# Output products of the dilated heads: one goes from the third latent pair to the last, and the last pair's three are tied to places in TensorE's order

## The chip, the cores and the metric

One core of a Trainium2 chip runs the kernel. The metric is device time in microseconds (us) of one execution. Engines are named as the profile names them: PE is TensorE (PEld its weight loads), DVE is VectorE, ACT is ScalarE, POOL is GpSimd, SP is SyncE.

## What is computed

A trunk of two layers over 512 tokens of width 1024. Each layer computes, in float32 (cut from the reference):

```python
h = rms_norm(x, g_norm_mix) * (1 + sc1) + sh1
q_d, k_d, v_d, cq, ckv, k_rope = split(h @ w_in)
o_dil = dilated_attention(...)      # 8 heads
o_mla = latent_attention(...)       # 8 heads
mix = concatenate([o_dil, o_mla]) @ w_out
x = x + gt1 * mix
h = rms_norm(x, g_norm_mlp) * (1 + sc2) + sh2
x = x + gt2 * (square(relu(h @ w_mlp_in)) @ w_mlp_out)
```

`x` is held transposed, as eight tiles `xT[j]` of 128 rows and 512 tokens. The product with `w_out` falls into a dilated half (the first 512 rows of `w_out`) and a latent half, and each half into eight output tiles j.

## The kernel before

**Precision.** A float32 weight tile is loaded into a `raw` buffer by SP's queue, copied by ACT to a rounded high part (`wh`), and POOL subtracts that from `raw` to give the low part `wl` (`load_split`, L229 to L238). A product of two such pairs is three matmuls: high by high, low by high, high by low (`mm3`, L240 to L245). There are 3 `raw`, 4 `wh` and 4 `wl` buffers, and 4 PSUM banks under the tag `mm`, 2 under `sc` and 2 under `tr`.

**Heads.** A layer runs its 16 heads as eight pairs, in the loop over `st` (0 to 7). Pairs 0 to 3 are dilated, pairs 4 to 7 latent; "third latent pair" is `st` 6, "last pair" `st` 7. `head` (L332 to L382) works through four query blocks: scores on TensorE, the maximum on DVE (L353), the exponential on ACT (L354), a normalising step that is on ACT (L358) for two blocks and on POOL (L362) for the other two, four transposes on TensorE (L365), and copies of the turned block by ACT (L370) and DVE (L371). After the four blocks comes the value product (L377), whose result ACT and DVE take out (L380, L381). At the end of a pair its output is split into `OT[st]` by ACT and POOL (L662, L663). While a pair runs, the queries, keys and values of the next pair are projected, normalised and transposed (`tail`, L636 to L645).

**Output products.** `out_dil(j)` (L697) is the whole dilated half of output tile j: four inner steps k of three matmuls each, 12 matmuls of 512 columns into one `mm` bank, and then a residual add of 512 columns on DVE (`add_x`, L670). It reads `OT[0]` to `OT[3]` (tiles named `ot` and `h` in the profile) and the weight tile `wo[0, j // 2]`; a weight tile serves two j. `early(j)` (L689) is the part of the latent half, on the first 256 tokens, that doesn't need the last pair: nine matmuls of 256 columns. The rest of the latent half follows when the last pair is done, then the norm, then the MLP.

**The order of the work.** The code traces the instructions in an order, and a planner then issues them: it walks a simulated time line, and on each engine takes, of the instructions that are ready, the one that was traced first. `heads` yields after each query block and after the value product, so five times for a head. `weave` (L708) fires the events of a pair between these yields: an event with position p fires at the first yield whose count i is greater than p. For `st` of 4 and more, `out_dil(2 * (st - 4))` stands at position 3.1 and `out_dil(2 * (st - 4) + 1)` at 5.1 (`OD0`, `OD1` in `TUNE`). The weight tiles of the dilated half are loaded at the end of the pairs 3 to 6 (`LO`, 7.2), those of the latent half in the last pair between 0.5 and 5 (`OL0`, `OL1`). `early(0)`, `early(1)` and `early(2)` stand at 5.5, 6.5 and 7.5 of the last pair, and `early(3)` to `early(6)` hang on hooks in its second head.

These positions give an instruction its rank, not its place. A place is fixed by `tc.keep_in_program_order(ins)`: it adds an edge from `ins` to the instruction of the same engine that was traced just before it, so that `ins` is issued behind that one. `mm3` does this for its first matmul where `pin` is true; `out_lat` and `early` pass it on for their first inner step.

In layer 0 the same stretch also carries blocks of the conditioning product (`mod_block`, L162 to L172) on DVE, or on POOL and ACT, which use `raw` buffers too.

Of the kernel before, what the change touches and what calls it, by code (L numbers as in the profile page):

```python
# [42 lines left out]
def trunk(ctx: ExitStack, tc: tile.TileContext, a):  # L43
    nc = tc.nc
    tn = lambda k: TUNE[k][min(lay[0], len(TUNE[k]) - 1)]
# [27 lines left out]
    def ps(tag, shape=(128, 512)):  # L73
        return psum.tile(list(shape), F32, tag=tag, bufs=BUFS[tag], name=nm(tag))
# [37 lines left out]
    for i in range(2):  # L112
        p = ps("sc", (128, 4, 128))
# [99 lines left out]
    def next_mod(**kw):  # L213
        if modq:
            modq.pop(0)(**kw)
# [24 lines left out]
    def mm3(out, sh, sl, mh, ml, first, last, pin=False):  # L240
        r = T.matmul(out, sh, mh, start=first, stop=False)  # L241
        if pin:
            tc.keep_in_program_order(r)
        T.matmul(out, sl, mh, start=False, stop=False)  # L244
        T.matmul(out, sh, ml, start=False, stop=last)  # L245
# [142 lines left out]
    for l in range(L):  # L388
# [6 lines left out]
        OT = []  # L395
# [259 lines left out]
        def heads(st, w):  # L655
            pr, bias = st % 4, (bias0 if l == 0 else True) if st < 4 else None
            o = s2(tag="o")
            for hd in range(2):
                hook = (lambda at: [early(j) for j in EARLY[at]]) if st == 7 and hd else (lambda at: None)
                yield from head(l, 2 * pr + hd, hd, w["score"], bias, w["vals"], o, hook)  # L660
            ot = t4("h" if st in (2, 3) else "ot", [128, 2, S])
            A.activation(ot[:, 0], o, AF.Copy)  # L662
            G.tensor_tensor(ot[:, 1], o, f(ot[:, 0]), op=OP.subtract)  # L663
            OT.append(ot)
# [4 lines left out]
        def add_x(j, hf, p, gt):  # L669
            V.scalar_tensor_tensor(xT[j][:, hf], p, gt[:, j:j + 1], xT[j][:, hf], op0=OP.mult, op1=OP.add)  # L670
# [3 lines left out]
        def out_load(half, jj):  # L674
            hi, lo = load_split(a["wout"][l, half, jj], 1024, tags=("zz", "zz") if half and jj == 3 else ("wh", "wl"))
            wo[half, jj] = (hi.rearrange("p (j k m) -> p j k m", j=2, k=4), lo.rearrange("p (j k m) -> p j k m", j=2, k=4))
# [12 lines left out]
        def early(j, pin=True):  # L689
            p = ps("mm")[:, :256]  # L690
            out_lat(j, p, HALF[0], (0, 1, 2), True, j < 4, pin)
            if j < 4:
                add_x(j, HALF[0], p, gt1)
            else:
                held[j] = p

        def out_dil(j):  # L697
            wh, wl = wo[0, j // 2]
            p = ps("mm")
            for k in range(4):  # L700
                mm3(p, wh[:, j % 2, k], wl[:, j % 2, k], OT[k][:, 0], OT[k][:, 1], k == 0, k == 3)
            add_x(j, slice(0, S), p, gt1)

        def run(events):
# [3 lines left out]
        def weave(main, events):  # L708
            ev = sorted(events, key=lambda x: x[0])
            i = 0  # L710
            for _ in main:
                i += 1
                while ev and ev[0][0] < i:
                    ev.pop(0)[1]()
            for _, fn in ev:
                fn()

        def spread(fns, p0, p1):
            return [(p0 + (p1 - p0) * i / max(1, len(fns) - 1), fn) for i, fn in enumerate(fns)]

        def flow(w, p0, p1):

            d = (p1 - p0) / 4
            ev = []
            for tb in range(4):
                b0 = p0 + d * tb
                ev += spread(w["mm"][tb], b0, b0 + 0.9 * d) + [(b0 + 0.95 * d, w["chain"][tb])]
            return ev
# [5 lines left out]
        if l == 0:  # L734
# [3 lines left out]
            p = ps("sc")  # L738
# [55 lines left out]
        else:  # L794
# [6 lines left out]
            ev = []  # L801
# [4 lines left out]
        for st in range(8):  # L806
            ev = []
            nx = PR.get(st + 1)
            if st == 0:
                if l == 0:  # L810
                    ev += spread(PR[1]["load"][2:], -2, -1)
                else:
                    ev += spread(PR[1]["load"], -2, -1)
            if st < 3:
                ev += flow(nx, tn("F0"), tn("F1")) + [(tn("T0"), nx["tail"][0]), (tn("T1"), nx["tail"][1])]
            elif nx:
                ev += flow(nx, tn("M0"), tn("M1")) + [(tn("M2"), nx["tail"][0]), (tn("M3"), nx["tail"][1])]
            if st < 2:
                ev += spread(PR[st + 2]["load"], tn("LD0"), tn("LD1"))
            elif st < 6:  # L820
                ev += [(tn("LM"), PR[st + 2]["load"][0])]
            if st >= 3 and st < 7:
                ev += [(tn("LO"), lambda jj=st - 3: out_load(0, jj))]
            if st >= 4:
                ev += [(tn("OD0"), lambda j=2 * (st - 4): out_dil(j)), (tn("OD1"), lambda j=2 * (st - 4) + 1: out_dil(j))]
            if st == 7:
                ev += spread([lambda jj=jj: out_load(1, jj) for jj in range(4)], tn("OL0"), tn("OL1"))
                ev += [(tn("OE") + j, lambda j=j: early(j)) for j in range(3)]
            if l == 0:
                on_dve = ("MV0", "MV1", "MV2", "MV3") if st < 3 else ("MV4", "MV5") if 4 <= st < 7 else ()  # L830
                on_pool = ("MP0", "MP1") if 4 <= st < 7 else ()
                ev += [(tn(x), lambda: next_mod(pin=True)) for x in on_dve]
                ev += [(tn(x), lambda: next_mod(pool_=True)) for x in on_pool]
            weave(heads(st, PR[st]), ev)
# [10 lines left out]
        for j in (4, 5, 6, 7, 0, 1, 2, 3):  # L845
            p = held[j] if j >= 4 else ps("mm")[:, :256]
# [4 lines left out]
        for j in range(8):  # L851
            p = ps("mm")[:, :256]
# [27 lines left out]
        for grp in ((0, 8), (8, 16), (16, 24), (24, 28), (28, 32)):  # L880
# [19 lines left out]
            if grp[1] - grp[0] == 8:  # L900
                for j in range(8):
                    w = tuple(t.rearrange("p (k m) -> p k m", k=8) for t in load_split(a["w2a"][l, grp[0] // 8, j], 1024))
                    p = ps("mm")
# [4 lines left out]
            else:  # L908
                gi = (grp[0] - 24) // 4
                ws = []  # L910
                for hf in ((FULL,) if gi == 0 else HALF):
                    n = hf.stop - hf.start
                    for j in range(8):
# [4 lines left out]
                        p = ps("mm")[:, :n]  # L918
# [70 lines left out]
```

## Time and profile before

| | |
|---|---|
| median of 3 runs | 1345.82 us (1344.32 to 1347.77) |
| profiled execution | 1343.71 us |
| its span, first to last instruction | 1341.6 us |
| PE, PEld busy | 1263.8 us (94%), 1108.2 us (83%) |
| DVE, ACT, POOL busy | 762.4, 679.8, 652.0 us |

The profile is one execution. Its time and its span differ by what lies around the first and the last instruction. Busy times of matmuls overlap a little, since they are pipelined: a busy PE is one that has no gap, and the distance between starts tells what one matmul takes.

### The profile page before, as it was taken

The numbers are of one execution on the slowest core, as the hardware profiler recorded it, in microseconds if no ns is written. First come the engines' busy times: TensorE is split into PE (matmuls) and PEld (weight loads), VectorE is DVE, ScalarE is ACT, GpSimd is POOL, SyncE is SP. The second block draws the span as 40 slices with busy tenths as digits, with TensorE's granted clock in tenths as the row PEclk, the third lists the DMA queues.
The fourth block names the chain that finished last, engine by engine and source line by source line (L and its number), as shares of the span: only waits on it lengthen the run. The fifth ranks groups of instructions, "written<-read, shape, count | busy, mean of one in ns | idle before, by whom it ended". The sixth has DMA issues, their size and how long they took to land.

```text
span 1341.6 us, 19641 instructions
## 1 busy us (share of the span) xinstructions
PE 1263.8 (94%) x7114; PEld 1108.2 (83%) x7114; DVE 762.4 (57%) x1644; ACT 679.8 (51%) x1421; POOL 652.0 (49%) x504
## 2 busy tenths in 40 slices
PE   4879988988999999999999999899899999999998
PEld 2878867877998888888899999798799888888888
DVE  6777797886763661834476678987672121121223
ACT  5567898777632322322237677887663232232321
POOL 5646876674534444444438333545452444444441
PEclk7989999999999999999999999999999999999999
DMA  9335543332254572844434244211121222232221
GB/s 340 113 100 174 184 156 110 105 122 69 79 176 166 192 250 95 278 166 161 166 121 131 77 135 123 86 48 63 40 72 64 95 95 96 96 106 96 94 95 64
DMA packets 57248, 167.62 MB, mean 125 GB/s; under 512 B 8640, under 2 KB 10816, under 8 KB 57152
## 3 DMA queue, kind: packets, MB, share of 16 engines
q1 hardware_dynamic: 57152, 166.38, 37.2%
q8 instruction: 56, 0.92, 0.3%
q14 instruction: 40, 0.33, 0.1%
HBM read 155.87 MB, written 10.49 MB: 124 GB/s over the span
## 4 chain that ended last, share of the span: by engine, by line
PE 75%; DVE 6%; ACT 5%; DMA 3%; POOL 3%; issue 2%; DVEq 0%; ACTq 0%; POOLq 0%
PE mm L241 22%; PE mm L244 22%; PE mm L245 22%; PE tr L377 3%; PE tr L365 2%; DMA raw<-in_wout_dram 1%; DVE pt L371 1%; POOL wl L234 1%; DVE P L350 1%; ACT P L354 1%; PE sc L241 1%; ACT wh L233 1%; POOL raw L167 1%; PE sc L244 1%; PE sc L492 1%
## 5 line engine op out<-in xcount | busy, mean ns | idle before, releaser
L234 POOL TENSOR_TENSOR wl<-raw,wh 128x1024 fp32r<-128x1024 f32 (+3 forms) x174 | 395.2, 2273 | 434.4 <-ACT wh L233 431.1
L233 ACT ACTIVATE wh<-raw 128x1024 fp32r<-128x1024 f32 (+3 forms) x174 | 174.7, 1004 | 264.7 <-PE mm L245 212.0
L670 DVE SCALAR_TENSOR_TENSOR x<-mm,mod,x 128x512 f32<-128x512 f32 (+1 forms) x152 | 92.4, 621 | 255.1 <-PE mm L245 254.5
L241 PE MATMUL mm<-h,wh 128*128 128x512 f32 (+1 forms) x544 | 198.3, 364 | 0.0
L244 PE MATMUL mm<-h,wl 128*128 128x512 f32 (+1 forms) x544 | 198.1, 364 | 0.0
L245 PE MATMUL mm<-h,wh 128*128 128x512 f32 (+1 forms) x544 | 197.9, 364 | 0.0
L241 PE MATMUL mm<-ot,wh 128*128 128x512 f32 (+1 forms) x416 | 147.1, 354 | 0.8 <-DVE x L670 0.4
L865 ACT ACTIVATE P<-mm 128x512 f32<-128x512 f32 (+1 forms) x80 | 41.0, 513 | 210.3 <-PE mm L245 206.8
L245 PE MATMUL mm<-ot,wh 128*128 128x512 f32 (+1 forms) x416 | 143.7, 349 | 1.5 <-POOL ot L663 1.5
L244 PE MATMUL mm<-ot,wl 128*128 128x512 f32 (+1 forms) x416 | 144.9, 349 | 0.0
L866 DVE SCALAR_TENSOR_TENSOR mm<-mm,P 128x512 f32<-128x512 f32 (+1 forms) x80 | 46.9, 589 | 135.7 <-ACT P L865 135.7
L241 PEld LDWEIGHTS mm<-h,wh 128*128 128x128 f32 x544 | 102.7, 189 | 16.3
L244 PEld LDWEIGHTS mm<-h,wl 128*128 128x128 f32 x544 | 102.7, 189 | 16.1
L245 PEld LDWEIGHTS mm<-h,wh 128*128 128x128 f32 x544 | 102.6, 189 | 16.2
L241 PE MATMUL mm<-qk,wh 128*128 128x512 f32 (+1 forms) x288 | 105.3, 366 | 1.0 <-DVE x L670 1.0
L244 PE MATMUL mm<-qk,wl 128*128 128x512 f32 (+1 forms) x288 | 105.3, 365 | 0.0
L245 PE MATMUL mm<-qk,wh 128*128 128x512 f32 (+1 forms) x288 | 105.2, 365 | 0.0
L170 DVE SCALAR_TENSOR_TENSOR pt<-pt,cb 128x1024 f32<-128x1024 f32 x56 | 100.7, 1828 | 0.0
L371 DVE TENSOR_TENSOR pt<-tr,pt 128x512 fp32r<-128x512 f32 x128 | 86.6, 684 | 18.1 <-ACT pt L370 17.5
L362 POOL TENSOR_SCALAR P<-P,hs 128x512 f32<-128x512 f32 x64 | 48.1, 751 | 99.9 <-DVE hs L355 81.0
L241 PE MATMUL mm<-wh,h 128*128 128x384 f32 x240 | 81.3, 353 | 11.7 <-ACT h L772 9.8
L365 PE MATMUL tr<-ident,P 128*128 128x128 f32 x512 | 77.5, 275 | 15.7 <-DVE o L381 6.1
(290 smaller groups left out, 2968.9 us busy)
## 6 DMA issues: line engine op xcount, KB each, us to landing
raw<-in_w_dram SPq DMA_DIRECT2D x64, 512.0 KB, 3.4
pt<-in_wmod_dram SPq DMA_DIRECT2D x56, 512.0 KB, 4.8
raw<-in_w2a_dram SPq DMA_DIRECT2D x48, 512.0 KB, 3.5
raw<-in_wmod_dram SPq DMA_DIRECT2D x24, 512.0 KB, 3.6
raw<-in_win_dram SPq DMA_DIRECT2D x30, 384.0 KB, 3.0
bias<-b SPq DMA_DIRECT2D x32, 256.0 KB, 2.1
raw<-in_wout_dram SPq DMA_DIRECT2D x16, 512.0 KB, 3.7
raw<-in_w2b_dram SPq DMA_DIRECT2D x16, 512.0 KB, 3.4
```

The source lines that it names most:

```text
L170: r = V.scalar_tensor_tensor(w, w, 1.0, cb, op0=OP.mult, op1=OP.mult, accum_out=out)
L233: ra = A.activation(hi, raw, AF.Copy)
L234: rg = G.tensor_tensor(lo, raw, f(hi), op=OP.subtract)
L241: r = T.matmul(out, sh, mh, start=first, stop=False)
L244: T.matmul(out, sl, mh, start=False, stop=False)
L245: T.matmul(out, sh, ml, start=False, stop=last)
L362: G.tensor_scalar(P, P, r_, 0.0, op0=OP.mult, op1=OP.add)
L365: T.transpose(tr[:, kc], P[:, kc * 128:(kc + 1) * 128], ident)
L371: V.tensor_tensor(lo, tr, f(hi), op=OP.subtract)
L670: V.scalar_tensor_tensor(xT[j][:, hf], p, gt[:, j:j + 1], xT[j][:, hf], op0=OP.mult, op1=OP.add)
L865: A.activation(r, p, AF.Relu)
L866: V.scalar_tensor_tensor(p, p, 0.0, r, op0=OP.max, op1=OP.mult)
```

## The change

A table `OD` replaces the two positions. For `st` 4 and 5 it gives the same events as before. For `st` 6 it leaves product 4 alone, at 4.1. For `st` 7 it has product 5 at 1.6, 6 at 3.1 and 7 at 4.6, and these three pass `pin`, so that the first matmul of each is tied to the instruction traced before it on TensorE: the transposes of the second block, the transposes of the fourth block and the value product of the pair's first head. Nothing is computed in another way.

```diff
-        def out_dil(j):
+
+        OD = {4: ((3.1, 0), (5.1, 1)), 5: ((3.1, 2), (5.1, 3)), 6: ((4.1, 4),), 7: ((1.6, 5), (3.1, 6), (4.6, 7))}
+
+        def out_dil(j, pin=False):
             wh, wl = wo[0, j // 2]
             p = ps("mm")
             for k in range(4):
-                mm3(p, wh[:, j % 2, k], wl[:, j % 2, k], OT[k][:, 0], OT[k][:, 1], k == 0, k == 3)
+                mm3(p, wh[:, j % 2, k], wl[:, j % 2, k], OT[k][:, 0], OT[k][:, 1], k == 0, k == 3, pin and k == 0)
             add_x(j, slice(0, S), p, gt1)
...
             if st >= 4:
-                ev += [(tn("OD0"), lambda j=2 * (st - 4): out_dil(j)), (tn("OD1"), lambda j=2 * (st - 4) + 1: out_dil(j))]
+                ev += [(at, lambda j=j, st=st: out_dil(j, st == 7)) for at, j in OD[st]]
```

## Rows read from the trace of the kernel before

**Rows 1.** The page, part 1: busy us, share of the span, instructions.
```profile
PE 1263.8 (94%) x7114; PEld 1108.2 (83%) x7114; DVE 762.4 (57%) x1644; ACT 679.8 (51%) x1421; POOL 652.0 (49%) x504
```

**Rows 2.** Busy time by stretch, layer 1: from:to, length, each engine's, granted clock, DMA.
```profile
898.20:912.10 13.90, 13.84 (x100) 12.52 (x99) 12.00 (x33) 12.00 (x35) 8.75 (x11) 1.00 0.24 77
912.10:928.90 16.80, 16.80 (x102) 14.65 (x101) 12.06 (x25) 12.19 (x23) 7.73 (x9) 1.00 0.19 63
928.90:937.50 8.60, 7.65 (x50) 6.05 (x49) 6.14 (x13) 7.25 (x16) 4.85 (x4) 1.00 0.18 61
937.50:945.80 8.30, 7.35 (x46) 5.65 (x45) 6.14 (x13) 6.80 (x15) 1.34 (x3) 1.00 0.01 2
945.80:955.70 9.90, 7.78 (x49) 6.08 (x48) 6.55 (x14) 8.26 (x17) 4.29 (x4) 1.00 0.00 0
955.70:965.00 9.30, 8.28 (x71) 8.04 (x70) 4.85 (x10) 5.28 (x10) 3.40 (x3) 1.00 0.27 86
```

**Rows 3.** The same view, layer 0 (order of engines: PE, PEld, DVE, ACT, POOL).
```profile
274.30:291.60 17.30, 17.30 (x102) 14.87 (x101) 13.04 (x28) 12.18 (x24) 13.58 (x20) 1.00 0.28 93
291.60:302.10 10.50, 7.55 (x46) 5.75 (x45) 9.05 (x15) 8.67 (x16) 10.36 (x6) 1.00 0.62 195
302.10:311.20 9.10, 7.84 (x49) 6.11 (x48) 6.20 (x13) 8.49 (x19) 3.76 (x3) 1.00 0.31 99
311.20:319.60 8.40, 7.03 (x46) 5.82 (x45) 6.78 (x14) 7.69 (x16) 2.63 (x3) 1.00 0.07 27
319.60:329.90 10.30, 9.06 (x73) 8.38 (x72) 5.37 (x11) 5.32 (x12) 6.14 (x4) 1.00 0.15 52
```

**Rows 4.** Timeline of PE in layer 1, second latent pair: start, length, instruction.
```profile
913.81 0.48 PE L241 MATMUL mm<-ot,wh 128*128 128x512 f32 x1
...
916.64 0.40 PE L241 MATMUL sc<-h,h 96*128 96x512 f32 x1
...
919.01 0.48 PE L241 MATMUL mm<-ot,wh 128*128 128x512 f32 x1
...
921.82 0.39 PE L241 MATMUL mm<-ot,wh 128*128 128x512 f32 x1
...
927.35 0.28 PE L241 MATMUL mm<-ot,wh 128*128 128x256 f32 x1
```

**Rows 5.** Timeline of PE, layer 1, last pair: idle before, and what ended it.
```profile
947.18 0.66 PE L365 MATMUL tr<-ident,P 128*128 128x128 f32 x4 [0.26 <-DVE o L381]
948.84 0.50 PE L241 MATMUL sc<-qk,qk 96*128 96x512 f32 x1 [1.00 <-ACT P L354]
...
957.14 0.66 PE L365 MATMUL tr<-ident,P 128*128 128x128 f32 x4 [1.02 <-DVE o L381]
```

**Rows 6.** The same, layer 0.
```profile
313.34 0.66 PE L365 MATMUL tr<-ident,P 128*128 128x128 f32 x4 [0.82 <-DVE o L381]
```

**Rows 7.** Instructions of L670: count, then duration in ns as min/median/max.
```profile
L670 DVE SCALAR_TENSOR_TENSOR x<-mm,mod,x x104: 467/485/754, 234.4 to 983.6; 128x256 f32<-128x256 f32 x56, 128x512 f32<-128x512 f32 x48
```

**Rows 8.** Timeline of ACT, layer 1, last head of the second latent pair.
```profile
912.14 0.59 ACT L380 ACTIVATE o<-tr 64x512 f32<-64x512 f32 x1 [1.40 <-PE tr L377]
...
916.84 1.06 ACT L233 ACTIVATE wh<-raw 128x1024 fp32r<-128x1024 f32 x1 [0.22 <-PE mm L245]
...
921.98 0.72 ACT L358 ACTIVATE P<-P,hs 128x512 f32<-128x512 f32 x1 [0.54 <-DVE hs L355]
924.28 0.60 ACT L370 ACTIVATE pt<-tr 128x512 fp32r<-128x512 f32 x1 [1.58 <-PE tr L365]
```

**Rows 9.** Timeline of POOL, layer 0, end of the second pair and third pair.
```profile
289.62 4.74 POOL L234 TENSOR_TENSOR wl<-raw,wh 128x1024 fp32r<-128x1024 f32 x2 [1.86 <-ACT wh L233]
...
296.56 0.71 POOL L362 TENSOR_SCALAR P<-P,hs 128x512 f32<-128x512 f32 x1
297.24 2.39 POOL L234 TENSOR_TENSOR wl<-raw,wh 128x1024 fp32r<-128x1024 f32 x1
```

**Rows 10.** Busy time by stretch, layer 0, dilated pairs, where the clock fell.
```profile
194.00:200.50 6.50, 2.84 (x12) 1.87 (x13) 5.70 (x19) 5.64 (x12) 6.50 (x8) 0.71 0.48 169
```

## The prediction

> **What bounds the kernel now.** I read the page first: TensorE is busy for 94% of the span, every other engine for 57% or less [rows 1]. So time is lost or won where TensorE idles, and where its work is put. The next view is the table of stretches for the six head bodies around the change, one for each head (each ends where the head's output copy L380 starts). In layer 1 the two heads of the second latent pair have TensorE busy 13.84 of 13.9 and 16.80 of 16.8 us; in the four heads of the third and last pairs it is busy 7.65 of 8.6, 7.35 of 8.3, 7.78 of 9.9 and 8.28 of 9.3 [rows 2]. [...] The reader is to see a full stretch, then four slack ones.
>
> The timeline of TensorE says why. The code puts products 4 and 5 into the third pair and 6 and 7 into the last one, but no edge holds them there, and the planner issues what is ready. All 512 column products of the dilated heads have run before the third pair begins: in layer 1 product 5 is at 913.81 to 916.64, 6 at 919.01, 7 from 921.82 to 927.35 (cut in two by heads' work) [rows 4]. Right behind it, at 927.35, stand three matmuls of `early(0)`: its pin ties it to the last matmul of product 7, which it was traced behind, and so it floats with it.
>
> **The change part by part.** *What it moves.* Product 5 leaves the third pair's list, 4 stays there unpinned, and 5, 6 and 7 are tied to the last pair: behind the second transposes, behind the fourth, and behind the value product of its first head. Product 4 I cost at nothing: it floats as before into idle TensorE time of the second pair (it ran there, in the 13.9 us stretch, and its weights don't change); if not, its 2.8 us land in the third pair's idle 1.9 us, and under 1 us shows. `early(0)` is now traced at a later position than product 7, so its pin comes to mean the first transposes of the last head, and the six of its nine matmuls that ran before the last pair go there too.
>
> *What it adds to the last pair.* The 12 matmuls of product 5 take 913.81 to 916.64, 2.83 us, or 0.24 from start to start [rows 4]. Three make 8.5. Six matmuls of 256 columns, at about half that pitch, make 0.7. So 9.2 us per layer. Against it stands TensorE's idle time there. In layer 1 it is 9.90 - 7.78 and 9.30 - 8.28, 3.1 us [rows 2]; the 0.26 ahead of the second transposes comes before product 5 may start and stays, the rest (1.00, 0.18, 0.68 and 1.02) [rows 5] lies behind a held product and can be filled: 2.9. In layer 0 idle is 1.37 + 1.24 = 2.6 [rows 3], of which the 0.82 ahead of the first transposes stays [rows 6]: 1.7. The last pair thus grows by 9.2 - 2.9 = 6.3 and by 9.2 - 1.7 = 7.5 us, 13.8 together. If the solid blocks starve ScalarE and VectorE and open new gaps, up to 1 us per layer comes on top; if nothing stays unfilled, 1 less.
>
> *What the second pair gives back.* Not the whole 8.5, since the next engine is close. In layer 1 ScalarE is busy 12.19 and VectorE 12.06 of the 16.8 us [rows 2]. With three residual adds at the 754 ns of a 512 column one gone, VectorE keeps 9.8 [rows 7]. ScalarE loses the copy of 1.06 at 916.84, whose buffer product 5 frees (it starts 0.2 us behind it). Following its order: from 912.14 to 916.84 it runs almost without a break, the removed copy ends at 917.9, from there to 921.4 there is again no break; the normalising at 921.98 and the last copy at 924.28, which waited 1.58 for TensorE, follow at once [rows 8]. The last copy would end about 922 and not 924.9, and the second half of the value product, which now waits for TensorE to finish product 7, would end about 923.5 and not 928.8. That is 5.3 less at best; I take 5, with 4 and 6 as ends.
>
> In layer 0 it is less, since GpSimd bounds this stretch: 13.58 of 17.3 and then 10.36 of 10.5 us [rows 3]. Two weight subtractions hold it from 289.62 to 294.36, and the normalising that the transposes wait for comes only at 296.56, behind a third piece of its work [rows 9]. Products 6 and 7 partly lay beside this. What comes earlier at the end of the second pair is met by the same queue in the third; the one relief is the subtraction of 2.39 at 297.24, which the change pushes into the last pair. I take 3.5, nearer to that 2.39 than to layer 1's 5, with 1 and 6 as ends.
>
> *The sum.* 13.8 - 5 - 3.5 = +5.3 us; with all ends, 11.8 - 12 = 0 and 15.8 - 5 = +11. The profiled execution took 1343.71 us, 2.1 less than the median of 1345.82; the sum gives 1349.0 there and **1351** on the median.
>
> *Queues that it is moved past.* The third weight tile of the latent half waits for product 5's buffer, now until the last pair. Its input tile, one of three, stays taken as long, so on SP the loads of MLP tiles 2 to 4 come one behind the other, and ScalarE's copies and GpSimd's 2.4 us passes for them move back too. I cost this at nothing: that third tile is first read by `early(4)` in the last head, about 10 us after product 5, and MLP tiles are read only behind the norm. Without that cover it costs up to one pass, 2.4 us a tile. The three residual adds wait on VectorE for their products, 0.75 us each with softmax steps behind them; VectorE is busy 6.55 of 9.9 and 4.85 of 9.3 us there [rows 2], so they hide.
>
> [...] Twelve starts 0.24 us apart and the next instruction right behind say that TensorE is full in the second pair [rows 4], and on this rests the largest give-back in the rivals. [...]
>
> **The rivals.** *TensorE alone set the second pair.* Its full stretches speak for it, and ScalarE and GpSimd would do weight copies elsewhere once free. Then 8.5 + 0.4 us come back in both layers, and the time is 13.8 - 17.8 = -4, **1342**. This decides if the second pair's last head falls below some 10 us in both layers. Against it: 9.8 us of VectorE and about 11 of ScalarE remain in layer 1, and 13.58 of GpSimd in layer 0.
>
> [...]
>
> *Nothing moves.* If an edge named an instruction that floats as well, as the pin of `early(0)` does, the products would stay where they are: 1346. The instructions ahead of these three hang on the last pair's softmax, so this is unlikely.
>
> **How the numbers follow.** Forecast 0.55, of which 0.10 lies under 4 us of growth; TensorE alone 0.28, of which 0.10 gains more than 4 (also by filling idle time in the third pair); the clock 0.09; nothing moves 0.03; another order by the planner, in no direction, 0.05. A change of 0.3% is 4 us, about what a measurement of this kernel can tell from none. Slower by more: 0.45 + 0.09 + 0.01 = 0.55. Faster by more: 0.10 + 0.03 = 0.13. Within: 0.32. The range is 1342 to 1356: from the rival's -4 to nearly the upper end of the sum, and the clock's case.
>
> **What would show it.** In the profile after: three blocks of 12 matmuls, 2.8 us each, in the first head of the last pair and behind it; that pair 25 to 27 us long with TensorE idle for under 1 us; the second pair's last head 11 to 13 us in layer 1 and 13 to 16 in layer 0, ScalarE and GpSimd near full; the third pair as before. It is wrong if that head falls below 10 us, if the last pair grows by less than 5 us, or if work from elsewhere fills the third pair.

## The result, and the profile after

The changed kernel takes 1357.35 us, the median of five runs (1351.84 to 1358.86), against 1345.82 before: a ratio of 1.0077, 95% interval 1.0052 to 1.0103, so slower by some 10 us. The forecast was 1351 in a range of 1342 to 1356: the direction came, the size is twice the forecast's, and the time lies outside the range.

The profiled execution took 1358.86 us (span 1357.1), 15.15 more than the 1343.71 before. Two views locate it. The first is the table of stretches. Layer 1 after the change: the six heads from the second latent pair to the last, then the stretch from the last head's output copy L380 to the MLP's first matmul. Columns as in [rows 2].

```profile
910.80:923.20 12.40, 11.29 (x90) 10.45 (x88) 10.64 (x30) 11.86 (x35) 8.07 (x10) 1.00 0.19 60
923.20:934.30 11.10, 11.04 (x72) 9.61 (x71) 10.37 (x26) 9.96 (x21) 4.40 (x8) 1.00 0.08 31
934.30:942.90 8.60, 7.49 (x47) 5.78 (x46) 6.63 (x14) 7.21 (x16) 4.17 (x5) 1.00 0.17 61
942.90:951.20 8.30, 7.36 (x46) 5.65 (x44) 6.15 (x13) 6.81 (x16) 1.31 (x3) 1.00 0.00 0
951.20:964.30 13.10, 12.83 (x72) 10.76 (x71) 7.96 (x15) 9.42 (x19) 5.31 (x5) 1.00 0.13 41
964.30:975.50 11.20, 11.20 (x89) 10.79 (x88) 5.93 (x11) 5.24 (x10) 4.80 (x2) 1.00 0.19 64
975.50:1000.60 25.10, 20.21 (x150) 19.28 (x148) 13.27 (x31) 12.29 (x22) 15.45 (x7) 0.93 0.36 122
```

The same for layer 0 after the change.

```profile
261.00:276.40 15.40, 12.97 (x83) 11.43 (x84) 13.39 (x34) 13.01 (x36) 9.11 (x12) 0.89 0.41 138
276.40:287.40 11.00, 10.89 (x71) 9.53 (x70) 8.21 (x21) 9.30 (x21) 8.06 (x13) 0.99 0.19 55
287.40:303.10 15.70, 10.05 (x51) 7.85 (x49) 11.20 (x21) 11.35 (x21) 11.67 (x13) 0.78 0.48 159
303.10:311.00 7.90, 7.17 (x42) 5.62 (x43) 6.86 (x15) 6.77 (x15) 3.56 (x4) 1.00 0.21 77
311.00:324.10 13.10, 12.83 (x72) 10.76 (x71) 7.84 (x15) 9.42 (x18) 5.30 (x5) 1.00 0.14 42
324.10:335.20 11.10, 11.10 (x88) 10.69 (x88) 5.74 (x11) 4.61 (x8) 5.49 (x3) 1.00 0.20 66
335.20:360.80 25.60, 21.53 (x149) 20.63 (x148) 13.18 (x31) 12.24 (x22) 15.45 (x7) 0.87 0.35 119
```

Before, three stretches that [rows 2, 3] don't hold: the second pair's first head of layer 0, and the way from the last output copy to the MLP in layers 0 and 1.

```profile
258.20:274.30 16.10, 13.98 (x96) 12.25 (x96) 14.17 (x36) 13.37 (x37) 9.81 (x13) 1.00 0.43 132
...
329.80:350.40 20.60, 18.46 (x150) 17.99 (x148) 12.70 (x31) 11.30 (x21) 13.23 (x7) 1.00 0.40 132
...
964.90:985.50 20.60, 18.44 (x149) 17.98 (x148) 12.73 (x31) 11.32 (x21) 13.20 (x6) 1.00 0.37 120
```

Added up, with [rows 2, 3]:

| stretch (us) | before | after | change | forecast |
|---|---|---|---|---|
| second and third pair, layer 0 | 53.0 | 50.0 | -3.0 | -3.5 |
| second and third pair, layer 1 | 47.6 | 40.4 | -7.2 | -5 |
| last pair, layer 0 | 18.7 | 24.2 | +5.5 | +7.5 |
| last pair, layer 1 | 19.2 | 24.3 | +5.1 | +6.3 |
| last output to MLP, layer 0 | 20.6 | 25.6 | **+5.0** | 0 |
| last output to MLP, layer 1 | 20.6 | 25.1 | **+4.5** | 0 |

The heads cost +0.4 in all, and 9.5 us appear behind them, where nothing was forecast. The other 5 us of this one profile lie mostly ahead of the second pair of layer 0 (which starts at 258.2 before and 261.0 after) and in layer 0's MLP and layer 1's start (423.7 us long before, 425.6 after), where TensorE's order is the same or nearly so and the clock fell at other places (its mean over 0 to 20 us is 0.81 before and 1.00 after, over 200 to 220 us 0.91 and 0.74, over the first 10 us of layer 0's MLP 1.00 and 0.83). They are not put down to the change: e4a and f1_layer1, kernels below that time like the one before, have 260.9 and 425.2, and 260.0 and 425.1, in their profiles.

The second view is TensorE's timeline behind the last pair of layer 1, with its idle time in brackets.

```profile
978.39 0.28 PE L245 MATMUL mm<-ot,zz 128*128 128x256 f32 x1
979.67 0.39 PE L241 MATMUL mm<-ot,wh 128*128 128x256 f32 x1 [1.00 <-ACT ot L662]
...
982.83 0.57 PE L245 MATMUL mm<-ot,wh 128*128 128x256 f32 x2 [1.94 <-POOL ot L663]
...
984.38 0.41 PE L245 MATMUL mm<-ot,wh 128*128 128x256 f32 x1
```

Two waits of 2.94 us together end with L662 and L663, the split of the last head output into its two parts. Neither wait exists before. In layer 0 the like waits are 0.23 and, at 341.82, 1.95. Then the clock falls, in layer 0 and in layer 1 (the table of stretches again):

```profile
341.80:348.20 6.40, 6.38 (x28) 6.15 (x29) 4.29 (x10) 2.06 (x5) 4.63 (x2) 0.50 0.55 188
...
983.10:986.50 3.40, 3.40 (x16) 3.14 (x16) 2.94 (x7) 0.80 (x2) 3.40 (x2) 0.50 0.45 158
```

The granted clock is 0.50, with TensorE busy 6.38 of 6.40 and 3.40 of 3.40 us. Its matmuls of 256 columns start 0.213 us apart there (layer 1, 984.17 to 986.30 for ten) and 0.119 apart at a clock of 1.00 right behind (986.65 to 987.96 for eleven). By an estimate from these two distances, 0.44 of the time is lost: of 3.40 that is 1.5 us, and 2.94 + 1.5 is 4.4, against the 4.5 measured. In layer 0: 0.23 + 1.95 of waiting and 2.8 of the 6.40 make 5.0, against 5.0.

Why L662 and L663 were late stands in the queues ahead of them. ScalarE, layer 1, after: the conversions L233 of weight tiles, and L662.

```profile
956.02 1.06 ACT L233 ACTIVATE wh<-raw 128x1024 fp32r<-128x1024 f32 x1 [0.65 <-PE mm L245]
...
963.21 1.06 ACT L233 ACTIVATE qk<-raw 128x1024 fp32r<-128x1024 f32 x1 [0.65 <-DMA raw<-in_w_dram]
...
970.17 1.06 ACT L233 ACTIVATE qk<-raw 128x1024 fp32r<-128x1024 f32 x1 [0.59 <-DMA raw<-in_w_dram]
...
975.47 0.59 ACT L380 ACTIVATE o<-tr 64x512 f32<-64x512 f32 x1 [2.40 <-PE tr L377]
978.04 1.06 ACT L233 ACTIVATE wh<-raw 128x1024 fp32r<-128x1024 f32 x1 [1.98 <-DMA raw<-in_w_dram]
979.01 0.61 ACT L662 ACTIVATE ot<-o 128x512 fp32r<-128x512 f32 x1
```

The copy at 956.02 is the third latent weight tile, released by product 5; before it ran at 916.84 [rows 8]. Its input buffer was taken until then, so MLP tiles 2, 3 and 4 came in one behind the other, at 963.21, 970.17 and 978.04, each awaited. Tile 4's copy waits 1.98 us for its DMA, and L662, whose input VectorE had ready at 976.78 (L381), stands behind it. GpSimd after:

```profile
979.18 2.38 POOL L234 TENSOR_TENSOR wl<-raw,wh 128x1024 fp32r<-128x1024 f32 x1 [5.46 <-ACT wh L233]
981.51 1.26 POOL L663 TENSOR_TENSOR ot<-o,ot 128x512 fp32r<-128x512 f32 x1
```

L663 stands behind tile 4's pass. Before, that pass had been done 3.8 us ahead of L663:

```profile
960.76 2.40 POOL L234 TENSOR_TENSOR wl<-raw,wh 128x1024 fp32r<-128x1024 f32 x1 [4.06 <-ACT wh L233]
966.98 1.29 POOL L663 TENSOR_TENSOR ot<-o,ot 128x512 fp32r<-128x512 f32 x1 [3.82 <-ACT ot L662]
```

From the output copy's start to L662 it was 1.34 us before (964.93 to 966.27, ScalarE) and is 3.54 now; to the end of L663 3.34 before and 7.30 now. So L662 comes 2.2 us later behind its output copy than before, and L663 starts at 981.51, as tile 4's pass ends (979.18 + 2.38), behind work that nobody waited for yet.

### The profile page after: what moved, and what is told of

Same layout as the page of the kernel before. It is cut to its first block, busy times and chain, and to the rows that moved or that the text cites. A ratio compares the mean times of both kernels' runs of the same rounds, so it can differ in the third digit from the quotient of the medians.

```text
span 1357.1 us, 19647 instructions
## 1 busy us (share of the span) xinstructions
PE 1275.6 (94%) x7114; PEld 1119.2 (82%) x7114; DVE 762.0 (56%) x1644; ACT 679.5 (50%) x1421; POOL 651.0 (48%) x504
## 4 chain that ended last, share of the span: by engine, by line
PE 72%; DVE 7%; ACT 5%; POOL 5%; DMA 4%; issue 3%; DVEq 0%; POOLq 0%; ACTq 0%
PE mm L241 21%; PE mm L245 21%; PE mm L244 21%; PE tr L377 2%; PE tr L365 2%; DMA raw<-in_w_dram 2%; POOL wl L234 1%; DVE pt L371 1%; DVE P L350 1%; PE mm L479 1%; POOL qk L234 1%; PE sc L241 1%; ACT wh L233 1%; PE sc L244 1%; PE sc L245 1%
## 5 line engine op out<-in xcount | busy, mean ns | idle before, releaser
L233 ACT ACTIVATE wh<-raw 128x1024 fp32r<-128x1024 f32 (+3 forms) x174 | 174.7, 1005 | 263.8 <-PE mm L245 209.1
L670 DVE SCALAR_TENSOR_TENSOR x<-mm,mod,x 128x512 f32<-128x512 f32 (+1 forms) x152 | 92.9, 622 | 264.3 <-PE mm L245 263.3
L241 PE MATMUL mm<-ot,wh 128*128 128x512 f32 (+1 forms) x416 | 148.6, 358 | 1.6 <-ACT ot L662 1.2
L245 PE MATMUL mm<-ot,wh 128*128 128x512 f32 (+1 forms) x416 | 145.6, 354 | 3.9 <-POOL ot L663 3.9
L371 DVE TENSOR_TENSOR pt<-tr,pt 128x512 fp32r<-128x512 f32 x128 | 86.8, 684 | 18.2 <-ACT pt L370 17.5
L241 PE MATMUL mm<-wh,h 128*128 128x384 f32 x240 | 82.3, 357 | 10.5 <-ACT h L775 8.5
L245 PEld LDWEIGHTS mm<-ot,wh 128*128 128x128 f32 x416 | 80.1, 194 | 14.4 <-POOL ot L663 4.3
```

The lines of the kernel that those rows point to most:

```text
L233: ra = A.activation(hi, raw, AF.Copy)
L371: V.tensor_tensor(lo, tr, f(hi), op=OP.subtract)
```

## The experiments

The theory after the comparison: holding product 5 keeps the third latent tile's input buffer, and with it MLP tile 4's load, back until its conversion lies across the last output's split. It is tested from both sides: free the buffer, or change the order. Where an expectation names a theory A, it is this one; theory B is that the last pair itself is too long.

**e1_rawh: another input buffer for that tile.**

```diff
-hi, lo = load_split(a["wout"][l, half, jj], 1024, tags=("zz", "zz") if half and jj == 3 else ("wh", "wl"))
+hi, lo = load_split(a["wout"][l, half, jj], 1024, raw="h" if half and jj == 2 else "raw", tags=("zz", "zz") if half and jj == 3 else ("wh", "wl"))
```

> The third latent weight tile (the one that waits for product 5's buffer) gets its input tile from another pool of buffers, so that all three raw buffers go on serving the MLP tiles. Theory A (late loads): what was lost behind the last pair comes from MLP tile 4, whose load is late because that raw buffer is held until product 5 has run; its copy on ScalarE and its subtraction on GpSimd then stand ahead of the last head's split. Then TensorE's waits behind the last pair (1.95 us in layer 0, 1.00 + 1.94 in layer 1) fall below 0.4 us each, and with the clock's falls that follow them the time goes from 1357 to 1347-1352. Theory B (the last pair itself is too long, and the rest is the clock's chance): waits and time stay, 1355-1358.

Measured: 1347.08, ratio 1.0008 (0.9994 to 1.0021). In layer 1 the way to the MLP is 20.60 again:

```profile
968.70:989.30 20.60, 18.43 (x150) 17.97 (x149) 12.77 (x31) 11.33 (x21) 13.20 (x6) 1.00 0.33 106
```

One buffer takes the loss away, as far as the times can tell, with products 5 to 7 where the change puts them.

**e4a: the buffer as in the change, but MLP tile 4 traced right behind tile 0 and tied in its place,** so that its passes cannot come between.

```diff
-ws1 = [w1_tile(i, i == 0) for i in range(4)]
+ws1 = {i: w1_tile(i, i in (0, 4)) for i in (0, 4, 2, 3, 1)}
...
-ws = ws1 + [w1_tile(i) for i in range(4, 8)] if grp[0] == 0 else []
+ws = [ws1[i] for i in range(5)] + [w1_tile(i) for i in range(5, 8)] if grp[0] == 0 else []
```

> The changed kernel with one difference: MLP tile 4 is traced right behind MLP tile 0 and tied to it on ScalarE and GpSimd, so that its copy and subtraction come behind the last head's split instead of ahead of it. The raw buffer stays held. Theory A: the waits behind the last pair go (below 0.4 us each) although the load is as late as before; 1348-1353. If the late load hurts in another way too (MLP waits for tile 4), a new wait appears in the MLP. Theory B: no change, 1355-1358.

Measured: 1347.45, ratio 1.0005 (0.9992 to 1.0018), half a microsecond under theory A's range, the way to the MLP 20.60 in both layers. Two different cures leave the same time; the loss is this queue. The layers' heads are nearly as in the change, 0.8 us above the kernel before in sum (0.4 in the table above), and that is what is left.

**f0_tie_before: the same tie in the kernel before,** as a control.

> The kernel before with the one edit that took the change's loss away: MLP tile 4 traced right behind tile 0 and tied in its place. Theory (the tie only mends the queue that the held product 5 upset; before, tile 4's GpSimd pass already lay ahead of the head outputs' last split): no difference, 1345 to 1348, last output to MLP start 20.6 us in both layers as before. Rival (the tie is a gain of its own, so that it flattered the change's kernel): 1341 to 1344, with other stretches than the one behind the last pair shorter by 2 us or more.

Measured: 1346.08, ratio 1.0002 (0.9989 to 1.0015). The tie gains nothing by itself; it only mends what the held product upset.

**e2_hold5: only product 5 tied.**

```diff
-OD = {4: ((3.1, 0), (5.1, 1)), 5: ((3.1, 2), (5.1, 3)), 6: ((4.1, 4),), 7: ((1.6, 5), (3.1, 6), (4.6, 7))}
+OD = {4: ((3.1, 0), (5.1, 1)), 5: ((3.1, 2), (5.1, 3)), 6: ((4.1, 4),), 7: ((1.6, 5), (3.1, 6), (5.1, 7))}
...
-ev += [(at, lambda j=j, st=st: out_dil(j, st == 7)) for at, j in OD[st]]
+ev += [(at, lambda j=j, st=st: out_dil(j, j == 5)) for at, j in OD[st]]
```

> Only product 5 is held in the last pair; 6 and 7 are unpinned at the positions of the kernel before and float into the second pair. Theory A: the raw buffer is held as in the changed kernel, so a wait of at least 1 us behind the last pair stays in each layer, though two of three products are back; 1349-1356. Theory B: a third of the loss, no wait behind the last pair, 1348-1350.

Measured: 1360.3, ratio 1.0099 (1.0082 to 1.0117): a miss in place and size. Products 6 and 7 did not go back to the second pair but ran behind 5 in the last one. Behind the last pair no such wait is left (20.5 us in both layers); the wait is now inside the last head, which is 17.0 us long in layer 0 and 16.0 in layer 1. ScalarE and TensorE there, layer 1:

```profile
968.49 1.06 ACT L233 ACTIVATE qk<-raw 128x1024 fp32r<-128x1024 f32 x1 [1.19 <-DMA raw<-in_w_dram]
969.45 0.70 ACT L358 ACTIVATE P<-P,hs 128x512 f32<-128x512 f32 x1
```

```profile
970.21 1.01 PE L365 MATMUL tr<-ident,P 128*128 128x128 f32 x4 [1.89 <-ACT P L358]
```

It is MLP tile 3's copy on ScalarE this time. It waits 1.19 us for its DMA, and behind it stands the normalising L358, whose input VectorE had ready at 967.49 (L355). The granted clock is lower in these heads too, 0.80 and 0.89. The same mechanism at another place; which step it hits depends on the order.

**e3_hold67: 6 and 7 tied, 5 back in the third pair's list,** untied.

```diff
-OD = {4: ((3.1, 0), (5.1, 1)), 5: ((3.1, 2), (5.1, 3)), 6: ((4.1, 4),), 7: ((1.6, 5), (3.1, 6), (4.6, 7))}
+OD = {4: ((3.1, 0), (5.1, 1)), 5: ((3.1, 2), (5.1, 3)), 6: ((3.1, 4), (5.1, 5)), 7: ((3.1, 6), (4.6, 7))}
```

> Product 5 goes back to the third pair's list, unpinned; 6 and 7 are held in the last pair. Theory A: product 5's buffers come free in the second pair, loads are early, no wait of over 0.4 us behind the last pair in either layer; what is left is heads against heads, 1343-1349. Theory B: two thirds of the loss, 1352-1355.

Measured: 1354.43, ratio 1.005 (1.0034 to 1.0065), outside what either theory gave. Behind the last pair all is as before, but in layer 1's third pair ScalarE holds MLP tile 2's copy ahead of L370, and TensorE waits:

```profile
933.91 1.06 ACT L233 ACTIVATE qk<-raw 128x1024 fp32r<-128x1024 f32 x1 [1.41 <-DMA raw<-in_w_dram]
935.00 0.60 ACT L370 ACTIVATE pt<-tr 128x512 fp32r<-128x512 f32 x1
```

```profile
936.32 0.50 PE L241 MATMUL sc<-h,h 96*128 96x512 f32 x1 [2.38 <-ACT P L354]
```

That head is 11.9 us instead of 8.6, with a granted clock of 0.86. So the theory had to widen: it is not product 5 as such. The order is fixed ahead by a planner, which here put conversions where their loads were still under way. In sum the last pairs are 4.6 and 4.1 us longer than before and the second and third pairs only 0.8 and 1.3 shorter (layer 0 and 1); layer 0's part was not followed further.

**e5_nopin: the change's list without its ties.**

```diff
-ev += [(at, lambda j=j, st=st: out_dil(j, st == 7)) for at, j in OD[st]]
+ev += [(at, lambda j=j, st=st: out_dil(j)) for at, j in OD[st]]
```

> The changed kernel's list of positions without the pins. Theory (the pins make the move; the list alone sets nothing, because the planner issues what is ready): products 5 to 7 run in the second pair again, its last head is about 17 us, the last pair 18 to 19, nothing waits behind it (20.6), 1345 to 1349. Rival (the traced position matters by itself, by the order in which buffers are handed out): the second pair's last head under 14 us, the last pair over 22 us, 1350 to 1358.

Measured: 1350.77, ratio 1.0037 (1.0026 to 1.0049), and both theories miss. Without ties the last pair is 19.2 us in layer 0, half a microsecond over [rows 3], so the ties do hold the products there. But the list alone keeps them out of layer 0's second pair: its last head is 11.1 us, and the third pair's first head takes them:

```profile
284.60:305.70 21.10, 18.03 (x88) 14.80 (x87) 12.81 (x26) 12.08 (x22) 16.23 (x15) 0.90 0.48 156
```

**f1_layer1: hold in layer 1 only,** with e4a's tie.

```diff
+if l == 0:
+    OD.update({6: ((3.1, 4), (5.1, 5)), 7: ((3.1, 6), (5.1, 7))})
...
-ev += [(at, lambda j=j, st=st: out_dil(j, st == 7)) for at, j in OD[st]]
+ev += [(at, lambda j=j, st=st: out_dil(j, l == 1 and st == 7)) for at, j in OD[st]]
```

> Products 5 to 7 held in layer 1 only, layer 0 in the list of before, and MLP tile 4 tied as in e4a. Theory (heads gain 2.1 us in layer 1 and lose 2.6 in layer 0, where GpSimd bounds): layer 0's six heads as before (about 71.6 us), layer 1's 64.7, 1343 to 1346, ratio 0.997 to 1.000. Rival (the 2.1 of layer 1 come from layer 0's shift, or go back elsewhere): layer 1's six heads at 66 us or more, 1346 to 1349.

Measured: 1345.04, ratio 0.9993 (0.9979 to 1.0006). The profile has the heads as expected, 71.6 us in layer 0 and 64.6 in layer 1, some 2.2 less than before [rows 2]. A gain of 2.2 is under what the times can tell.

**f2_layer1_pin4: f1_layer1 with product 4 tied too** (`st >= 6` in place of `st == 7`).

> f1_layer1 (products 5 to 7 held in layer 1 alone) with product 4 held in the third pair too. Theory (in the second pair TensorE sets the length, as it did for 5 to 7, and idles 1 us per head in the third): the second pair gives back 1 to 2.8 of product 4's 2.8 us, the third pair grows by 0.9 to 1.9, 1343 to 1345.5. Rival (ScalarE, busy 11.9 of 12.4 us in the second pair's first head of the changed kernel, sets that head once products 5 to 7 are gone, so that it gives nothing back): the second pair as in f1_layer1 (23.5 us together), the third pair 1 to 3 us longer, 1346 to 1348.

Measured: 1344.81, ratio 0.999 (0.9978 to 1.0002). The tie left every engine's order as in f1_layer1, presumably since the work that product 4 is tied behind floats as well, so this tells nothing of product 4; it is a second timing of f1_layer1.

**f7_pin4: product 4 really moved to the third pair:** f2_layer1_pin4 with a later position for it.

```diff
-OD = {4: ((3.1, 0), (5.1, 1)), 5: ((3.1, 2), (5.1, 3)), 6: ((4.1, 4),), 7: ((1.6, 5), (3.1, 6), (4.6, 7))}
+OD = {4: ((3.1, 0), (5.1, 1)), 5: ((3.1, 2), (5.1, 3)), 6: ((5.1, 4),), 7: ((1.6, 5), (3.1, 6), (4.6, 7))}
```

> f1_layer1 (products 5 to 7 held in layer 1 alone) with product 4 held in the third pair, behind the value product of its first head; in f2_layer1_pin4 the pin left every engine's order as it was. Theory (TensorE, busy 11.1 of 11.2 us in the second pair's last head, sets that head's length): that head falls by 1.5 to 2.8 us to 8.4 to 9.7, the third pair grows by 1 to 2; layer 1's six heads 63 to 65 us against 64.6, 1343 to 1346. Rival (ScalarE, busy 10 of 11.1 us there, sets it as soon as TensorE has less): that head at 10 us or more, the third pair 1 to 3 us longer, layer 1's heads 65.5 to 67, 1345 to 1348.

Measured: 1345.55, ratio 0.9991 (0.9979 to 1.0004). The second pair's last head and the third pair's second, layer 1:

```profile
913.80:923.70 9.90, 7.92 (x54) 6.50 (x53) 8.79 (x23) 8.72 (x20) 3.48 (x8) 1.00 0.08 34
...
932.30:942.40 10.10, 9.98 (x63) 8.39 (x62) 7.00 (x14) 6.75 (x15) 3.20 (x3) 1.00 0.17 52
```

The head gives 1.3 us (11.2 to 9.9) where TensorE loses 3.2 (11.14 to 7.92), and the third and last pair take 2.7 us back: layer 1's heads are 66.0 us, as the rival had it; the head itself lies between the two theories' bounds. With products 5 to 7 gone TensorE was still the limit there; with 4 gone too it no longer is (it waits 0.76 us for ScalarE's L641 and 1.19 for VectorE's L371), and moving it gains nothing.

**f3_gr2 and f4_tables: why layer 0's third pair lost 5 us in its first head.** In e4a GpSimd waits there for a small row of the next layer's key rotation. f3_gr2 gives that row a second buffer.

```diff
-g = const.tile([128, NR], F32, tag="gr", name=nm("gr"))
+g = const.tile([128, NR], F32, tag="gr1" if l and is_k else "gr", name=nm("gr"))
```

> e4a with a second buffer for the small gains row of layer 1's key rotation. In e4a, as in the changed kernel, GpSimd waits some 2 us for that row's DMA in the third pair's first head of layer 0, ahead of a weight subtraction and of the normalising that the transposes wait for. Theory (GpSimd's queue is what makes that head 15 to 16 us long instead of 10.6): that head shrinks by 2 to 4 us, to 12 to 14, 1343 to 1346. Rival (the head is long because what moves earlier meets ScalarE's or VectorE's own work, or the clock's fall, and the row's wait is only in line): that head at 15 us or more, 1346 to 1349.

Measured: 1355.27, ratio 1.0062 (1.0047 to 1.0076). It settles nothing: the key's table moved up to 86.3 us, far ahead of the latent pairs, and the order changed from there on (the second pair's heads are 19.9 and 13.8 us). f4_tables keeps the tables' first operation in its coded place instead.

```diff
-G.tensor_tensor(C[:, :, 0], cos, ga, op=OP.mult)
+(tc.keep_in_program_order if l else id)(G.tensor_tensor(C[:, :, 0], cos, ga, op=OP.mult))
```

> e4a with the first operation of layer 1's two sets of rotation tables kept in its coded place (layer 1's start), which takes the key's table, with its wait for a DMA of some 2 us and 1.8 to 3 us of GpSimd work, out of the third pair's first head in layer 0; nothing else of that head's order moves. Theory (GpSimd's queue makes that head long): the head falls from 16.0 us to 12 to 14, TensorE's wait for the normalising there from 2 us to under 1; the table's 1.8 us of work beside layer 1's first norm cost 0 to 1.5; 1343.5 to 1347. Rival (the wait is only in line, and the head's length comes from the weight tiles' own DMAs and passes, or from the clock): the head at 15 us or more, 1347 to 1349.

Measured: 1345.97, ratio 0.9995 (0.9984 to 1.0005). GpSimd in e4a, then TensorE in e4a and in f4_tables:

```profile
290.87 0.32 POOL L511 TENSOR_TENSOR rot<-cos,gr 128x64 f32<-128x64 f32 x1 [2.31 <-DMA gr<-in_gkr_dram]
...
296.60 0.69 POOL L362 TENSOR_SCALAR P<-P,hs 128x512 f32<-128x512 f32 x1
```

```profile
297.35 1.11 PE L365 MATMUL tr<-ident,P 128*128 128x128 f32 x4 [2.84 <-POOL P L362]
```

```profile
292.81 0.50 PE L241 MATMUL sc<-h,h 96*128 96x512 f32 x1 [2.71 <-ACT P L354]
...
294.31 1.06 PE L365 MATMUL tr<-ident,P 128*128 128x128 f32 x4 [0.52 <-DVE pt L371]
```

TensorE's wait ahead of these transposes falls from 2.84 to 0.52 and the head from 15.9 to 14.1, a touch over the 12 to 14 expected. The table in the queue was part of that head's length. The other 3.6 us over [rows 3] were not taken apart by a run. In the trace stand TensorE's wait of 2.71 us for an exponential that ScalarE reaches at 291.96 after 4.6 us without a break, a weight tile's copy among them, and a granted clock of 0.88 over the head (0.79 in e4a).

**f8_both: f7_pin4 with f4_tables.**

> f7_pin4 with layer 1's rotation tables kept in layer 1's start, as in f4_tables. Theory (GpSimd sets the second and third pair of layer 0, busy 13.58 of 17.3 and 10.36 of 10.5 us before): those two heads, 27.7 us together in f1_layer1, fall by 1 to 3 us, 1342 to 1345. Rival (with products 5 to 7 in the second pair TensorE sets its last head, and the tables' work of some 4 us lies beside it): the two heads at 27 us or more, the time as f7_pin4's within 1 us.

Measured: 1344.73, ratio 0.9987 (0.9976 to 0.9998), the smallest ratio of all. The two heads of layer 0 stay at 28.0, so the rival held and the tables cost nothing where TensorE is full beside them (busy 17.20 of 17.2 us in the second pair's last head). It beats the kernel before by 1.8 us, less than the 0.3% that was set as the bound.

## Why the prediction was wrong, by its steps

**Queues that it is moved past: the step that failed.** The text saw the chain (the third tile waits for product 5's buffer, its input tile stays taken, MLP tiles 2 to 4 load one behind the other, copies and passes move back) and cost it at nothing, since "MLP tiles are read only behind the norm". That asks who reads the tile. The question it left out is who stands behind its conversion on ScalarE and GpSimd: L662 and L663, which TensorE waits for. The cover named was there for the tiles themselves (TensorE waits for none of them in the last head), and not for what stood behind them. The price given for the case without cover, one pass of 2.4 us, was near the waits (2.9 in layer 1, 2.2 in layer 0). On top came the clock's fall. 9.5 us in all by the profile, and e1_rawh and e4a, which take it away, return to 1347.

**The clock.** The forecast gives the clock a chance of 0.09 and counts its case in the upper end of the range; no run shows that term. What stood in the rows was a mean granted clock of 0.71 in one stretch of layer 0 [rows 10]. The profile after shows 0.50 behind the last pair, after the new waits, which by the estimate above costs some 1.5 us in layer 1 and 2.8 in layer 0. The clock also fell in the third pair of layer 0, after a wait of 2.69 us:

```profile
294.00:300.00 6.00, 4.02 (x17) 3.29 (x16) 3.52 (x7) 2.86 (x5) 6.00 (x5) 0.50 0.44 142
```

The cost there is about 1 us, an estimate: from 297.05 to 300.97 four transposes and the value product take 3.92 us, and in the kernel before 2.96 (0.36, 1.50 and 1.10). In e1_rawh and e4a the clock falls there too (0.78 and 0.79 over the head) and stays at 1.00 behind the last pair.

**The last pair: right in kind, too dear.** Products 5, 6 and 7 run there in three blocks, from 952.97, 957.31 and 963.47 in layer 1, and TensorE is idle for 0.27 us. The blocks take 2.85, 2.85 and 2.76 us, as priced. Yet TensorE's busy time grew by 8.0 (16.06 to 24.03) and not by 9.2 (which work of the pair takes less is not shown), and with the idle time filled the pair grew by 5.1 and 5.5, not 6.3 and 7.5. `early(0)` went behind the last head's first transposes, as forecast.

**The second pair, layer 1: too little.** ScalarE was taken for the next limit, at 5 us. The pair gave 7.2. Its last head fell by 5.7 (16.80 to 11.10) and TensorE's busy time there by 5.76: TensorE had set that head alone, as the rival said. One thing that the text cost at nothing lies beneath: product 4 did not stay in the first head. Before, then after:

```profile
908.19 0.50 PE L241 MATMUL mm<-ot,wh 128*128 128x512 f32 x1
```

```profile
926.63 0.50 PE L241 MATMUL mm<-ot,wh 128*128 128x512 f32 x1
```

So the last head lost some 8.9 us of work and took 2.8 in, and the first head lost 2.8 and fell by 1.5 (13.9 to 12.4). There TensorE is the limit no longer: it waits 1.11 us for VectorE's L371, with ScalarE busy 11.86 of the 12.4. A next limit, which the forecast looked for in the last head, shows in the first.

**Layer 0: the net is right, the way to it in part.** The second pair gave 7.0 and the third took 4.0 back, 3.0 net against 3.5. But the signs named were a last head of 13 to 16 us in the second pair and a third pair as before, and it is 11.0, with 15.7 instead of 10.5 for the third pair's first head. TensorE there:

```profile
293.50 0.70 PE L241 MATMUL sc<-h,h 96*128 96x512 f32 x1 [2.69 <-ACT P L354]
...
297.05 1.12 PE L365 MATMUL tr<-ident,P 128*128 128x128 f32 x4 [1.98 <-POOL P L362]
```

The second wait is GpSimd's queue, as forecast, though with the table and its DMA in it (f4_tables), which the text did not have. The first and longer one is ScalarE's, and the clock falls behind it. That the net lies so near is in part luck.

So the heads' sum was +5.3 in the forecast and +0.4 in the profile, with errors of 5.4 us on one side and 0.5 on the other, and the step at nothing was worth 9.5. The two partly cancel, and neither shows in the difference of the end alone. Each engine's part of the move was priced; the part that was priced by a reason ("read later") and not by a row is the one that failed.

## What to carry to other kernels

When a change holds a buffer longer, follow it to the loads behind it, to their conversions, and then to whatever stands behind those conversions on their engines, needed or not; a tile that nobody reads yet can still block a step that everyone waits for (here tile 4's copy, and L662 2.2 us later). An order planned ahead is only as good as its guess of when loads land (in e3_hold67 a copy waited 1.41 us for its load, and TensorE 2.38 behind it), so tie the few conversions that would lie across a critical step to a place where nothing waits (e4a: 20.60 us to the MLP again). And where an engine is full in one head and idle in the next, moving work is worth what the first gives back less what the second cannot hide: here -3.0 and -7.2 against +5.5 and +5.1 (layer 0 and 1), nearly a draw.

## What was unexpected of the hardware

The clock can fall or stay behind one and the same work. At the MLP's start of layer 1 TensorE is idle for 1.94 us (3.40 - 1.46) in the kernel before as in f1_layer1, its instructions from the last output copy on are the same in the same order, and the first stretch has 12 matmuls, 1.46 of 3.40 us, in both. Before:

```profile
983.50:986.90 3.40, 1.46 (x12) 1.40 (x12) 3.26 (x9) 1.81 (x4) 1.52 (x3) 1.00 0.49 146
986.90:990.30 3.40, 3.40 (x31) 3.40 (x30) 2.98 (x8) 2.61 (x6) 3.23 (x6) 1.00 0.05 22
```

f1_layer1:

```profile
984.80:988.20 3.40, 1.46 (x12) 1.40 (x12) 3.27 (x9) 1.81 (x4) 1.56 (x3) 1.00 0.40 133
988.20:991.60 3.40, 3.40 (x18) 3.40 (x17) 2.99 (x8) 2.62 (x6) 3.23 (x6) 0.50 0.06 25
```

The granted clock behind it is 1.00 in one and 0.50 in the other, and 18 matmuls run in the time of 31. Whether such spells make the runs of one kernel scatter by several us is open: the mean granted clock of an execution does not tell its time, since of the kernel before executions of 1342.88 and of 1348.78 us both have 0.99.
